# Stick-breaking weights from two sigmoids instead of Abs, Exp, Ln and Exp, one written order over four head pairs, and four gate tiles made as seven-product pairs

## The chip, the cores and the metric

The kernel runs on one core of one Trainium2 chip. The metric is the device time of a run in microseconds; it is given as the median of several runs with the lowest and the highest. A profile is one further execution, recorded by the hardware profiler. The engines are PE (TensorE, with PEld for its weight loads), DVE (VectorE), ACT (ScalarE), POOL (GpSimd) and SP (which issues most of the loads).

## The reference

One layer of a streaming encoder on 1024 prompt rows and 32 sample rows (1056 together), width 1024, all in fp32. One product with `w_in` gives the latents of branch A (latent attention), q, k and v of branch B (stick-breaking attention, 8 heads of 64) and two gates; then come both attentions, the gated merge, and a feed-forward part. The change lies in branch B and in the product with `w_in`:

```python
p = h @ w_in
q_lat, c_kv, k_r, q_b, k_b, v_b, g_a, g_b = jnp.split(p, IN_SPLITS, axis=-1)

def sb_attend(q, qpos, k, v, kpos):
    z = jnp.einsum('bqhd,bshd->bhqs', q, k).astype(jnp.float32) * SB_SCALE
    mask = kpos[None, :] < qpos[:, None]
    sp = jnp.where(mask, jax.nn.softplus(z), 0.0)
    later = lax.cumsum(sp, axis=3, reverse=True) - sp
    a = jnp.where(mask, jnp.exp(jax.nn.log_sigmoid(z) - later), 0.0)
    return jnp.einsum('bhqs,bshd->bqhd', a.astype(v.dtype), v)
```

A weight is thus exp(z - softplus(z) - the sum of softplus over the later keys that are allowed), which is the same number as sigmoid(z) times the product of sigmoid(-z) over those later keys. The prompt's attention takes 1024 queries with 1024 keys; the sample rows take 32 queries with 512 cached keys and their own 32.

## The kernel before

**Products.** Every fp32 operand is held as a high part (rounded to fp32r by ACT, `hi`, L68) and a low part (what is left, by DVE, `lo`, L71), so a product is three matmuls: high by high, low by high, high by low (L75 to L77, or L2207 to L2209 in `prod`). A tile of 128 columns of `w_in` against the 1056 rows is done in one of two ways. Plain: three blocks of 352 rows (`BLK`), 8 x 3 = 24 matmuls each. As a pair: two tiles together as seven products of half-size quarters (`pair`, L595), in the manner of Strassen's scheme; a product is 12 matmuls of 256 and 12 of 272 columns (`HB`), and ACT and DVE make the sums and splits of quarters around it (`half`, `plus`, L538 to L640).

**Stages.** `stage_qkv` makes the first q tile, the first k tile and one latent tile plainly, then the ten others of q, k and v as five pairs. `stage_sb` (L1162) does the prompt's stick-breaking attention for four head pairs, one after the other, and beside it the 16 gate tiles, plainly: 384 steps of three matmuls that fill PE between the pieces of attention. `stage_lat` (L1278) and what stands around it do the other latents, the norms of latents (`lat_norm`, `lat_rstd`, L1236 to L1275) and the sample rows' stick-breaking (`sb_sample`, `sb_weights`, L824 to L842), in two passes of four heads. Then follow the latent attention, merge, and feed-forward.

**Order in SB.** In `stage_sb` PE, ACT and DVE run in a written order (`manual_schedule`), a table of tokens `ORDER` for one head pair, used four times. A token is a letter with a tile: of head `h`, block of 256 queries `u` and half `i`, and behind it `a` or `b` for half a tile. `S` is the scores on PE (L1211, L1212, into PSUM tiles `s`); `a`, `e`, `l`, `E` are the ACT passes Abs, Exp, Ln and Exp (L746, L748, L750, L766); `x`, `c`, `d` are on DVE the maximum with 0 plus the logarithm (L752), the running sum from the last key to the first (L756, L759) and the difference (L764); `k` copies a carry. Then `T` transposes the weights on PE (L807), `h` and `v` split them, `V` multiplies with the values (L821), `o` and `p` gather, and POOL stores the output (L1005). `f` is one step of a gate tile, `W` and `w` split the next weight tile, `G` takes a finished block of a gate tile out of PSUM (L1132) and POOL stores it to the scratch tensor `gd` (L1133). `A`, `D` and `Q` are pieces of a small product for the next norm. Loads of Q, K and V for the next head or pair hang on certain tokens (`then`); they go out on SP.

**Tables of ACT.** The kernel begins with a table of functions that is chosen by name (L130), and ACT changes it only at L1719 and L2352. In `sb_weights` the sample rows go through the same passes (L831 Abs, L832 Exp, L833 Ln, L834 to L841 on DVE, L842 Exp), and each norm of latents takes its inverse root as Identity, Ln, Exp and Square on ACT (L1242 to L1245), then three steps on DVE (L1246 to L1248).

**Buffers.** The weights of the attention lie in tiles with the tag `A` (five buffers); "big" is another tag with three buffers of 1056 numbers, in a pool that lives past SB. `wr`, `wh`, `wl` (the raw weights and their two parts) have two buffers each.

Of the kernel before, what the change touches and what calls it, by code (L numbers as in the profile page):

```python
# [8 lines left out]
F32 = mybir.dt.float32  # L9
# [8 lines left out]
P = 128  # L18
# [26 lines left out]
class K:  # L45
# [82 lines left out]
    def consts(self):  # L128
# [317 lines left out]
    def stage_qkv(self):  # L446
# [3 lines left out]
        nc, a = self.nc, self.a  # L450
        Tp = self.tc.alloc_tile_pool(name="sums", bufs=1, side="right", reuse_waits="tile")
# [58 lines left out]
        def after(kind, p, u):  # L510

            x = u[:, :TP]
            low = x.bitcast(F32R)
            if kind == "q":
                QH = sg() if p == 1 else flat(T4[0])[:, TP * (p - 2) : TP * (p - 1)]
                self.hi(QH, x, 0.125)
                nc.scalar.mul(self.qsb[:, p], u[:, TP:T], 0.125)
                spill("qh", p, QH)
                with self.tc.issue_after(self.plus):
                    stt(low, x, 0.125, fl(QH), ALU.mult, ALU.subtract)  # L520
                spill("ql", p, low)
                return
# [72 lines left out]
        def pair(i, ta, tb, ua, ub):  # L595
# [37 lines left out]
            if i < 4:  # L633
                raws.append((raw(col(*pairs[i + 1][0])), raw(col(*pairs[i + 1][1]))))
# [17 lines left out]
        col = lambda kind, p: 672 + 512 * "qkv".index(kind) + p * P  # L652
        pairs = ((("v", 0), ("v", 1)), (("k", 1), ("q", 1)), (("k", 2), ("k", 3)), (("v", 2), ("v", 3)), (("q", 2), ("q", 3)))
# [34 lines left out]
        self.in_w.append(self.w_in_tile(2208))  # L688
# [27 lines left out]

    def sb_attend(self, score, V, out, fill, then):
        nc = self.nc
        act, vec = nc.scalar.activation, nc.vector
        tiles, banks, seen = {}, {}, {}  # L720
        common = self.sums(V, out, tiles)
        todo = None
        for x in self.ORDER:
            if todo:
                todo()
            todo = then.get(x)
            k, x = x[0], x[1:]
            if k in "fGDQWwA":
                for _ in range(int(x or 1)):
                    fill(k)  # L730
                continue
            h, u = divmod(int(x[0]), 4)
            if k in "SaelxckdE":
                n, i, part = x[0], int(x[2]), x[3:]
                w = (2 * u + i + 1) * P
                m = w // 2 if part else w
                c0 = m if part == "a" else 0
                if k == "S":
                    if part != "b":
                        tiles[x[:3]] = self.tl(self.At, [P, TP], F32, "A")  # L740
                    banks[x] = self.tl(self.ps, [P, 512], F32, "s")
                    score(h, banks[x], 2 * u + i, c0, max(m, 256))
                    continue
                ps, A = banks[x][:, :m], tiles[x[:3]][:, c0 : c0 + m]
                if k == "a":
                    act(A, ps, AF.Abs)  # L746
                elif k == "e":
                    act(A, A, AF.Exp, scale=-1.0)  # L748
                elif k == "l":
                    act(A, A, AF.Ln, bias=1.0)  # L750
                elif k == "x":
                    vec.scalar_tensor_tensor(A, ps, 0.0, A, ALU.max, ALU.add)  # L752
# [14 lines left out]
                continue  # L767
            common(k, x, h, u)
# [264 lines left out]
    def sample_load(self, b):  # L1033

        nc, a = self.nc, self.a
        if b:
# [6 lines left out]
        self.ck, self.cv = self.tl(self.sm2, [P, TP], F32, "A"), self.tl(self.sm2, [P, BIG], F32, "big")  # L1043
        for x, c in ((self.ck, "k"), (self.cv[:, :TP], "v")):
# [54 lines left out]
    def gates(self):  # L1099
# [3 lines left out]
        w, ps, ada = [self.w_in_tile(2208)], [], []  # L1103
# [1650 lines left out]
```

## Time and profile before

| what | us |
|---|---|
| median of 3 runs | 1677.44 |
| lowest, highest | 1676.64, 1681.24 |
| the profiled execution, its span | 1673.5 |
| stage of pairs, 80.6 to 190.5 | 109.9 |
| SB and gates, 190.5 to 500.4 | 309.9 |
| sample rows and latents, 500.4 to 583.0 | 82.6 |

The page and the answers of the trace give no time of the profiled execution other than its span. The boundaries are those that I read from the lines of the first and last instruction of a stage. In a timeline a row is the start in us, the duration in us, the engine, the line, the operation, out<-in, shapes, and in brackets the idle time before with what ended it. In a table of groups, the last columns are busy us, mean ns of one, and idle time before with what ended most of it.

### The profile page before, as it was taken

To read this page: it belongs to the slowest core of one execution; us is meant where nothing else is said; L and a number is where in the kernel's file an instruction comes from. 1 tells how busy PE (TensorE), PEld (TensorE's weight loads), DVE (VectorE), ACT (ScalarE), POOL (GpSimd) and SP (SyncE) were. 2 spreads that over 40 slices of the span, in tenths; PEclk is the share of its full clock that TensorE was granted. 3 is DMA by queue.
4 is the path that set the end of the run, shared out by engine and by line. 5 is a ranking of instruction groups with operands and counts; after the bars stand their busy time and mean duration, and the time that the engine had idled before them with its cause. 6 is when DMAs were issued, how large, how long until landed. Compare 5 with 4: busy or idle time off the path is not lost. (4 is left out here: it accounts for less than half of the span.)

```text
span 1673.5 us, 30264 instructions
## 1 busy us (share of the span) xinstructions
PE 1636.1 (98%) x11592; PEld 1505.2 (90%) x11592; DVE 1268.7 (76%) x2140; ACT 1007.4 (60%) x1945; POOL 297.8 (18%) x581
## 2 busy tenths in 40 slices
PE   5999999999999999999999999999999999999996
PEld 3999999999998889998988799999999999877885
DVE  4865698989873689987765889878778778787455
ACT  4544687978874589887762675544444444454442
POOL 2113312111121221111000212212112111200013
PEclk8999999999999999999999999999999999999998
DMA  9345875576542533222474423432332332796643
GB/s 337 108 131 181 293 232 166 166 198 178 179 126 63 169 105 87 84 87 63 150 256 138 160 89 120 133 133 95 133 133 95 133 133 95 256 331 234 201 141 117
DMA packets 194145, 260.62 MB, mean 156 GB/s; under 512 B 23374, under 2 KB 132304, under 8 KB 193936
## 3 DMA queue, kind: packets, MB, share of 16 engines
q1 hardware_dynamic: 172944, 198.50, 38.2%
q0 software_dynamic: 20688, 59.56, 10.2%
q8 instruction: 91, 1.49, 0.4%
q10 hardware_dynamic: 368, 0.63, 0.1%
q14 instruction: 54, 0.44, 0.1%
HBM read 191.11 MB, written 67.82 MB: 155 GB/s over the span
## 5 line engine op out<-in xcount | busy, mean ns | idle before, releaser
L68 ACT ACTIVATE wh<-wr 128x1024 fp32r<-128x1024 f32 (+2 forms) x151 | 130.1, 864 | 226.6 <-PE s L2208 86.6
L71 DVE TENSOR_TENSOR wl<-wr,wh 128x1024 fp32r<-128x1024 f32 (+2 forms) x151 | 148.5, 986 | 79.3 <-ACT wh L68 79.1
L75 PE MATMUL mm<-hh,wh 128*128 128x352 f32 x456 | 152.6, 335 | 0.0
L76 PE MATMUL mm<-hl,wh 128*128 128x352 f32 x456 | 148.7, 326 | 0.0
L77 PE MATMUL mm<-hh,wl 128*128 128x352 f32 x456 | 148.4, 326 | 0.0
L2207 PE MATMUL mm<-T,wh 128*128 128x256 f32 (+1 forms) x376 | 108.3, 288 | 0.0
L2209 PE MATMUL mm<-T,wl 128*128 128x256 f32 (+1 forms) x376 | 107.3, 286 | 0.4 <-DVE wl L71 0.2
L2208 PE MATMUL mm<-T,wh 128*128 128x256 f32 (+1 forms) x376 | 106.8, 284 | 0.0
L2209 PE MATMUL s<-T,wl 128*128 128x256 f32 (+1 forms) x348 | 99.4, 286 | 0.0
L2207 PE MATMUL s<-T,wh 128*128 128x256 f32 (+1 forms) x348 | 99.4, 286 | 0.0
L2208 PE MATMUL s<-T,wh 128*128 128x256 f32 (+1 forms) x348 | 98.9, 284 | 0.0
L71 DVE TENSOR_TENSOR wl<-S,wh 128x1024 fp32r<-128x1024 f32 (+1 forms) x55 | 59.2, 1078 | 51.8 <-ACT wh L68 51.4
L75 PEld LDWEIGHTS mm<-hh,wh 128*128 128x128 f32 x456 | 86.5, 190 | 3.3 <-issue 2.1
L76 PEld LDWEIGHTS mm<-hl,wh 128*128 128x128 f32 x456 | 86.5, 190 | 2.4 <-issue 0.8
L2348 DVE SCALAR_TENSOR_TENSOR u<-u,c,u 128x1058 f32<-128x1058 f32 x68 | 87.1, 1318 | 2.0 <-ACT u L2345 0.7
L807 PE MATMUL tr<-c,A 128*128 128x128 f32 x576 | 87.2, 272 | 0.0
L77 PEld LDWEIGHTS mm<-hh,wl 128*128 128x128 f32 x456 | 86.4, 189 | 0.2
L68 ACT ACTIVATE wh<-S 128x1024 fp32r<-128x1024 f32 (+1 forms) x55 | 51.8, 943 | 47.6 <-PE s L2208 13.0
L2207 PE MATMUL tr<-T,wh 128*128 128x272 f32 (+1 forms) x272 | 77.9, 286 | 0.0
L2209 PE MATMUL tr<-T,wl 128*128 128x272 f32 (+1 forms) x272 | 77.7, 286 | 0.0
L2208 PE MATMUL tr<-T,wh 128*128 128x272 f32 (+1 forms) x272 | 77.4, 284 | 0.0
L2338 POOL COPY c<-u 128x2 f32<-128x2 f32 x44 | 26.7, 607 | 263.5 <-DVE u L2284 227.6
(770 smaller groups left out, 5832.5 us busy)
## 6 DMA issues: line engine op xcount, KB each, us to landing
wr<-in_w_up_dram SPq DMA_DIRECT2D x44, 512.0 KB, 4.0
dr<-in_w_down_dram SPq DMA_DIRECT2D x43, 512.0 KB, 5.0
wr<-in_w_in_dram SPq DMA_DIRECT2D x33, 512.0 KB, 6.3
A<-in_w_ada_dram SPq DMA_DIRECT2D x32, 512.0 KB, 5.8
wr<-gdn SPq DMA_DIRECT2D x30, 512.0 KB, 4.5
gdn<-u POOLq DMA_DIRECT2D x23, 512.0 KB, 4.9
gd<-nat POOLq DMA_DIRECT2D x48, 176.0 KB, 3.6
t<-gd SPq DMA_DIRECT2D x16, 528.0 KB, 5.1
```

The costliest lines, as they stand in the source:

```text
L68: self.nc.scalar.activation(out, in_, AF.Identity, scale=scale)
L71: return self.nc.vector.tensor_tensor(out, full, hi.bitcast(F32), ALU.subtract)
L75: m(ps, lh, rh, start=start, stop=False)
L76: m(ps, lh, rl, start=False, stop=False)
L77: self.pe = m(ps, ll, rh, start=False, stop=stop).ins
L807: self.nc.tensor.transpose(tr[:, (2 * s + q) * P : (2 * s + q + 1) * P], at[q][:, b * P : b * P + P], self.idt)
L2207: m(ps[:, :n], w[0][:, k], x[0][:, k, c], start=first and k == 0, stop=False, skip_group_check=True)
L2208: m(ps[:, :n], w[0][:, k], x[1][:, k, c], start=False, stop=False, skip_group_check=True)
L2209: i = m(ps[:, :n], w[1][:, k], x[0][:, k, c], start=False, stop=k == 3, skip_group_check=True)
L2338: nc.gpsimd.tensor_copy(self.CV[:, 0:2, cc], u[:, 1024:1026])
L2348: nc.vector.scalar_tensor_tensor(y, u[:, w : w + YW], self.cvT[:, w, cc : cc + 1], y, ALU.mult, ALU.add)
```

## The change

**Sigmoids.** In SB two ACT passes read the scores from PSUM: sigmoid(z) into the tile `A` and sigmoid(-z) into a second tile `rest` with the tag "big". The running sum becomes a running product from the last key to the first (a constant tile `one`, zero with an identity in it, both starts it and keeps it at 1 up to the mask). One multiplication of `A` with the tile `rest`, shifted by one key, gives the weight. For the shift the column behind the last key is set to 0 by a POOL memset, one for each of the 64 tiles. The letters `l`, `x`, `k`, `E` are gone; `a`, `e`, `c`, `d` remain. The sample rows' `sb_weights` and the norms keep their Abs, Exp and Ln.

**One order.** `ORDER` is one table for all four head pairs, so that the pieces of two pairs can mix; a token carries its pair. The loads of Q and K (`L`), and V (`Y`), and of other things (`F`, `Z`) are tokens of their own; `B` replaces a step that hung on the gate blocks. All of these stand at new places.

**Gates.** `GATES = 4`: gate tiles 0 to 3 are made in `stage_qkv` as two more pairs, between the pairs (v2, v3) and (q2, q3), and each is stored whole to `gd` by POOL. The tiles 4 to 15 stay in SB as 288 steps.

```diff
+        self.one = cv.bitcast(BF16)
+        nc.vector.memset(self.one, 0.0)
+        nc.vector.tensor_copy(self.one[:, 384:512], self.idt)
...
+            if kind == "g":
+                self.gsent = nc.gpsimd.dma_start(self.gd[p], u).ins
+                return
...
-        pairs = ((("v", 0), ("v", 1)), (("k", 1), ("q", 1)), (("k", 2), ("k", 3)), (("v", 2), ("v", 3)), (("q", 2), ("q", 3)))
+        pairs = [(("v", 0), ("v", 1)), (("k", 1), ("q", 1)), (("k", 2), ("k", 3)), (("v", 2), ("v", 3))]
+        pairs += [(("g", m), ("g", m + 1)) for m in range(0, self.GATES, 2)]
+        pairs.append((("q", 2), ("q", 3)))
...
+    GATES = 4
...
-        S0.0 a0.0 f1 S0.1 f1 a0.1 e0.0 S1.0 f1 l0.0 f1 e0.1 f1 a1.0 l0.1 e1.0 f1 x0.0 c0.0 f1 d0.0 E0.0 f2 S2.0a
...
-                if k == "a":
-                    act(A, ps, AF.Abs)
-                elif k == "e":
-                    act(A, A, AF.Exp, scale=-1.0)
-                elif k == "l":
-                    act(A, A, AF.Ln, bias=1.0)
-                elif k == "x":
-                    vec.scalar_tensor_tensor(A, ps, 0.0, A, ALU.max, ALU.add)
...
-                elif k == "d":
-                    vec.tensor_tensor(A, ps, A, ALU.subtract)
                 else:
-                    act(A, A, AF.Exp)
...
+            elif k == "a":
+                act(tiles[p][t][:, c], banks[x][:, :m], AF.Sigmoid)
+            elif k == "e":
+                if (p, t) not in rest:
+                    rest[p, t] = self.tl(self.sm2, [P, BIG], F32, "big")
+                    nc.gpsimd.memset(rest[p, t][:, w : w + 1], 0.0)
+                act(rest[p, t][:, c], banks[x][:, :m], AF.Sigmoid, scale=-1.0)
+            elif k == "c":
+                R = rest[p, t]
+                r = R[:, c][:, ::-1]
+                if part == "b":
+                    vec.tensor_tensor_scan(r, r, r, R[:, m : m + 1], ALU.mult, ALU.bypass)
                 else:
+                    vec.tensor_tensor_scan(r, r, self.one[:, 512 - m : 512][:, ::-1], 0.0, ALU.mult, ALU.add)
+            else:
+                A = tiles[p][t][:, c]
+                vec.tensor_tensor(A, A, rest[p, t][:, c0 + 1 : c0 + m + 1], ALU.mult)
...
-            for m in range(16):
+            for m in range(self.GATES, 16):
```

By the order of the instructions the rows of PE go from 10702 to 10750 (288 matmuls of 352 columns fewer, 336 of 256 or 272 more), those of ACT from 1773 to 1601, of DVE from 2104 to 1996, of POOL from 547 to 604 (64 memsets more; 36 stores of blocks and four of whole tiles in place of 48 of blocks), and ACT's loads of a table from 3 to 13. Behind SB the rows of PE and DVE are as before.

The first place is ACT in the first pass of the sample rows, in the stage behind SB. `A` holds the weights of the sample rows, `wr` and `wh` the next weight tile, `lt` and "big" a latent. Before:

```order
L831 ACTIVATE A_6330<-s_6322 128x272
L831 ACTIVATE A_6330<-s_6325 128x272
L832 ACTIVATE A_6330<-A_6330 128x272 x2
L833 ACTIVATE A_6330<-A_6330 128x272 x2
L68 ACTIVATE wh_6376<-wr_6374 128x1024
L68 ACTIVATE wh_6620<-wr_6618 128x1024
L842 ACTIVATE A_6330<-A_6330 128x272
L1304 COPY lt_6245<-s_6347 128x352
L1269 ACTIVATE big_6560<-lt_6245 128x352
L842 ACTIVATE A_6330<-A_6330 128x272
```

Now (the lines count 40 more, those of the latents 53 more):

```order
L871 ACTIVATE A_6175<-s_6167 128x272
L871 ACTIVATE A_6175<-s_6170 128x272
L872 ACT_TABLE_LOAD
L872 ACTIVATE A_6175<-A_6175 128x272 x2
L873 ACT_TABLE_LOAD
L873 ACTIVATE A_6175<-A_6175 128x272 x2
L68 ACTIVATE wh_6221<-wr_6219 128x1024
L1357 COPY lt_6090<-s_6192 128x352
L68 ACTIVATE wh_6465<-wr_6463 128x1024
L1322 ACTIVATE big_6405<-lt_6090 128x352
L882 ACT_TABLE_LOAD
L882 ACTIVATE A_6175<-A_6175 128x272 x2
```

Two loads of a table now stand ahead of the split of the weight tile, and one ahead of the last pass; two of the four other steps changed places.

The second place is ACT in the second pass of the sample rows and the first norm of latents behind it. Before:

```order
L833 ACTIVATE A_6514<-A_6514 128x272 x2
L1269 ACTIVATE nat_6570<-lt_6373 128x352
L842 ACTIVATE A_6514<-A_6514 128x272 x2
L1014 COPY A_6532<-tr_6533 128x512
L1017 COPY A_6532<-tr_6539 32x128
L1242 ACTIVATE A_6581<-mm_6575,c_76 128x264
L1243 ACTIVATE A_6581<-A_6581 128x264
L1244 ACTIVATE A_6581<-A_6581 128x264
```

Now:

```order
L873 ACT_TABLE_LOAD
L873 ACTIVATE A_6359<-A_6359 128x272 x2
L1322 ACTIVATE nat_6415<-lt_6218 128x352
L882 ACT_TABLE_LOAD
L882 ACTIVATE A_6359<-A_6359 128x272 x2
L1054 COPY A_6377<-tr_6378 128x512
L1057 COPY A_6377<-tr_6384 32x128
L1295 ACTIVATE A_6426<-mm_6420,c_76 128x264
L1296 ACT_TABLE_LOAD
L1296 ACTIVATE A_6426<-A_6426 128x264
L1297 ACT_TABLE_LOAD
L1297 ACTIVATE A_6426<-A_6426 128x264
```

The steps stand as before, with a load of a table ahead of every one of these groups of Ln and of Exp.

The third place is POOL at the start of SB, where `ptd` are two constant tiles, `gd` the gates' scratch, `nat` a finished gate block, `ob` the output of a head and "big" the tiles of sigmoid(-z). Before:

```order
L1159 MEMSET ptd_2211 128x128
L1159 MEMSET ptd_2212 128x128
L1133 DMA gd<-nat_2327 128x352
L1133 DMA gd<-nat_2366 128x352
L1005 DMA ob_2181<-o_2436 64x256
L1133 DMA gd<-nat_2475 128x352
```

Now:

```order
L1203 MEMSET ptd_2649 128x128
L1203 MEMSET ptd_2650 128x128
L797 MEMSET big_2740 128x1
L797 MEMSET big_2743 128x1
L797 MEMSET big_2774 128x1
L1175 DMA gd<-nat_2708 128x352
L797 MEMSET big_2780 128x1
L797 MEMSET big_2808 128x1
L1175 DMA gd<-nat_2802 128x352
L797 MEMSET big_2848 128x1
L797 MEMSET big_2855 128x1
L797 MEMSET big_2900 128x1
```

The memsets of new tiles stand in one queue with the stores of gate blocks.

More of the change, by code (lines that the diff above doesn't have):

```diff
@@ L632, in pair @@
             w5 = half(s2b)
-            if i < 4:
+            if i < len(pairs) - 1:
                 raws.append((raw(col(*pairs[i + 1][0])), raw(col(*pairs[i + 1][1]))))
@@ L715, with sb_attend @@
+        3S7.1b 3v7.3 3V6.1 3a7.1b f 3e7.1b Z 3V6.0 f 3c7.1b 3o6 f 3T7.2 3p6 3d7.1b f 3h7.2 3V7.3 3v7.2 3T7.1 3V7.2
+        3h7.1 3T7.0 3v7.1 f 3h7.0 f 3v7.0 3V7.1 B 3V7.0 Q f 3o7 3p7 G
     """.split()
-    def sb_attend(self, score, V, out, fill, then):
+    def sb_attend(self, score, common, fill, load):
         nc = self.nc
         act, vec = nc.scalar.activation, nc.vector
-        tiles, banks, seen = {}, {}, {}
-        common = self.sums(V, out, tiles)
-        todo = None
+        tiles, banks, rest = [{} for _ in range(4)], {}, {}
+        common = [f(tiles[p]) for p, f in enumerate(common)]
@@ L723, in sb_attend @@
         for x in self.ORDER:
[L724 to L730, printed above, removed]
+            if not x[0].isdigit():
+                for _ in range(int(x[1:] or 1)):
+                    fill(x[0])
+                continue
+            p, k, x = int(x[0]), x[1], x[2:]
+            if k in "LY":
+                load(k, p, int(x))
@@ L1031, in pv_sample, with sample_load @@
                                       pv[64 * h : 64 * h + 64, 32 * h : 32 * h + 32])
-    def sample_load(self, b):
+    def sample_load(self, b, part="kv"):
         nc, a = self.nc, self.a
-        if b:
+        if b and part == "k":
             x = self.tl(self.sm2, [P, TP], F32, "A")
@@ L1042, in sample_load @@
         hs = slice(4 * b, 4 * b + 4)
-        self.ck, self.cv = self.tl(self.sm2, [P, TP], F32, "A"), self.tl(self.sm2, [P, BIG], F32, "big")
-        for x, c in ((self.ck, "k"), (self.cv[:, :TP], "v")):
+        for c in part:
+            if c == "k":
+                x = self.ck = self.tl(self.sm2, [P, TP], F32, "A")
+            else:
+                self.cv = self.tl(self.sm2, [P, BIG], F32, "big")
+                x = self.cv[:, :TP]
             self.load(x.rearrange("p (t c) -> p t c", t=4),
@@ L1119, in steps @@
                             yield
-                    if b == 1 and self.ada_sum is not None:
-                        ada.append(self.ada_turn())
                     yield
@@ L1201, in stage_sb @@
                 self.tl(self.sm2, [P, w], F32, g)
-        self.ahead = self.gate_raw(1)
+        self.ahead = self.gate_raw(self.GATES + 1)
         self.sent = self.wlast
@@ L1214, in stage_sb, with fill, load, common @@
         fill = self.gates()
-        E = mybir.EngineType
-        for p in range(4):
-            then = {"S2.0a": lambda: queries(p, 1), "S2.1a": lambda: values(p, 1)}
-            if p == 0:
-                then["S2.1a"] = lambda: (values(p, 1), self.ada_fetch(4, self.sm2))
-            if p < 3:
-                then.update({"S3.1b": lambda: queries(p + 1, 0), "V3.0": lambda: values(p + 1, 0)})
-            with self.tc.manual_schedule(engines={E.PE, E.Activation, E.DVE}):
-                self.sb_attend(score, lambda b, h: V[h][:, b * P : b * P + P], self.store(self.obd[p]), fill, then)
+        gate = fill
+        def fill(k):
+            if k == "F":
+                self.ada_fetch(4, self.sm2)
+            elif k == "Z":
+                self.sample_load(1, "v")
+            else:
+                gate(k)
+        def load(k, p, h):
+            (queries if k == "L" else values)(p, h)
+        def common(p):
+            return lambda tiles: self.sums(lambda b, h: V[h][:, b * P : b * P + P], self.store(self.obd[p]), tiles)
+        E = mybir.EngineType
+        with self.tc.manual_schedule(engines={E.PE, E.Activation, E.DVE}):
+            self.sb_attend(score, [common(p) for p in range(4)], fill, load)
         self.in_w.append(self.next_w.pop(0))
```

131 lines of the change are left out of this document (79 added, 52 removed).

## The prediction

> **What bounds the kernel now.** I read the page first, then the table of stages, then the groups of ScalarE (ACT) and VectorE (DVE), then the timeline at the places that the change touches. The page's own lines on the span and on TensorE (PE):
>
> ```profile
> span 1673.5 us, 30264 instructions
> PE 1636.1 (98%) x11592; PEld 1505.2 (90%) x11592; DVE 1268.7 (76%) x2140; ACT 1007.4 (60%) x1945; POOL 297.8 (18%) x581
> ```
>
> The span is 1673.5 us; the median of the three runs is 1677.44 us (1676.64 to 1681.24), so 3.9 us lie around the span, and I carry them along unchanged. PE is busy 98% of the span, so a change counts here if it takes work off PE or makes PE wait. The stages that the change touches, in the table of stages (length of the stage, then busy time of PE, weight loads, DVE, ACT, POOL, then the granted clock and the DMA share): the products for q, k and v in pairs; stick-breaking (SB); the sample rows and the latents.
>
> ```profile
> 80.60:190.50 109.90, 109.90 (x911) 109.56 (x910) 63.61 (x107) 50.90 (x110) 29.56 (x50) 1.00 0.56 172
> 190.50:500.40 309.90, 309.90 (x2244) 297.31 (x2243) 268.64 (x470) 257.79 (x564) 60.88 (x116) 1.00 0.65 189
> 500.40:583.00 82.60, 81.33 (x622) 73.23 (x620) 40.62 (x85) 41.19 (x86) 16.19 (x32) 1.00 0.40 111
> ```
>
> In the first two PE is busy from end to end at the full clock. DVE is at 87% and ACT at 83% in SB, and yet PE never stands still for them. So what the sigmoids save on ACT and DVE is worth nothing by itself: it only pays if it lets PE do less. The third stage is another matter. ACT is busy there for only half of the time, but it works in chains whose end PE waits for.
>
> **The sigmoids.** Four ACT passes and three DVE passes for a piece of weights become two and two. The groups of before in SB:
>
> ```profile
> L748 ACT ACTIVATE A<-A 128x384 f32<-128x384 f32 (+5 forms) x96 | 50.3, 524 | 1.1
> L746 ACT ACTIVATE A<-s 128x384 f32<-128x384 f32 (+5 forms) x96 | 46.8, 488 | 15.1 <-PE s L1212 14.7
> L752 DVE SCALAR_TENSOR_TENSOR A<-s,A 128x384 f32<-128x384 f32 (+5 forms) x96 | 52.7, 549 | 18.7 <-ACT A L750 18.3
> ```
>
> A sigmoid read from PSUM stands in no row; the nearest are 488 ns (the pass that reads PSUM) and 524 ns (one that doesn't), and I take 488. The other two passes of before (L750, L766) have the same shapes, so ACT loses four passes of some 47 to 50 us and gains two of 47: about 100 us less in SB. DVE loses the 52.7 us of the maximum; the scan and the last step stay, with a product in place of a sum or a difference. Both leave PE's path as they found it, at 0 us. What covers that is PE's own queue; if the cover were gone, the new wait would be a rival (below).
>
> **Four gate tiles in pairs.** Here PE's work changes. A gate tile was three blocks of 24 matmuls of 352 columns. Two of them become seven products of 24 matmuls, 12 of 256 columns and 12 of 272. PE's rows in the timeline, one block of 352 columns behind some transposes, and one product:
>
> ```profile
> 501.18 0.41 PE L75 MATMUL s<-hh,wh 128*128 128x352 f32 x1
> 501.42 0.32 PE L76 MATMUL s<-hl,wh 128*128 128x352 f32 x1
> ...
> 504.97 0.32 PE L77 MATMUL s<-hh,wl 128*128 128x352 f32 x1
> ...
> 101.09 0.28 PE L2207 MATMUL mm<-hh,wh 128*128 128x256 f32 x1
> ...
> 102.53 0.29 PE L2207 MATMUL mm<-hh,wh 128*128 128x272 f32 x1
> ...
> 104.03 0.28 PE L2207 MATMUL s<-hh,wh 128*128 128x256 f32 x1
> ```
>
> The second column must not be used as the price, since neighbours overlap. From start to start, 22 steps of 352 columns take 504.97 - 501.42 = 3.55 us, so 161 ns each; a product takes 104.03 - 101.09 = 2.94 us. Two gate tiles cost 144 x 0.161 = 23.2 us, a pair 7 x 2.94 = 20.6 us. Two pairs save 2 x 2.65 = 5.3 us on PE. The pairs' splits and sums on ACT and DVE lie beside that: in the first stage they are busy 46% and 58%, and the pairs there with more work behind them (v and k go out in natural order) leave PE no gap. The four larger stores of gates sit on POOL's queue, which has the same number of bytes to send as before.
>
> The first matmul behind a transpose takes 0.24 us to the next start (501.18 to 501.42), 0.08 more than the others. By the order of the instructions PE goes from transposes to such a matmul 73 times in SB, 68 times before: +0.4 us.
>
> **What the sigmoids bring along.** In the order of after, ACT loads a table of functions ten more times: once at the first sigmoid, ahead of the first scores and behind eleven steps of gate matmuls, so hidden (1.3 us of ACT if it were not); and nine times where Exp and Ln come back, five in the two sample passes (L832, L833, L842), four in the two norms of latents (L1243, L1244). Before, one table served all of these. The price of a load, from ACT's timeline at another place, where it also stands between two instructions:
>
> ```profile
> 820.56 0.36 ACT L793 COPY o<-pv 64x256 f32<-64x256 f32 x1 [0.16 <-DVE V L71]
> 820.94 1.28 ACT L1719 ACT_TABLE_LOAD   x1
> 822.24 0.20 ACT L1719 ACTIVATE ss<-c 128x1 f32<-128x1 f32 x1
> ```
>
> 820.94 to 822.24 is 1.30 us; the overlap that two ACT instructions otherwise have (about 0.1 us) goes too, so I take 1.4 us a load. The Trainium skill (page "ScalarE: Activation LUTs", section "What ACT_TABLE_LOAD costs") puts a switch at 2.66 us, as 1.28 us of load and 1.38 us of draining; by that the stalls below would double. The 20 ns between the load's end and the next start do not show such a drain.
>
> First sample pass, ACT's rows, DVE's, PE's:
>
> ```profile
> 506.21 0.76 ACT L831 ACTIVATE A<-s 128x272 f32<-128x272 f32 x2
> 506.87 0.74 ACT L832 ACTIVATE A<-A 128x272 f32<-128x272 f32 x2
> 507.51 0.74 ACT L833 ACTIVATE A<-A 128x272 f32<-128x272 f32 x2
> 508.15 1.05 ACT L68 ACTIVATE wh<-wr 128x1024 fp32r<-128x1024 f32 x1
> ...
> 507.96 0.79 DVE L834 SCALAR_TENSOR_TENSOR A<-s,A 128x272 f32<-128x272 f32 x2 [0.63 <-ACT A L833]
> 508.78 0.73 DVE L836 TENSOR_TENSOR_SCAN A<-A 128x272 f32<-128x272 f32 x1
> 509.42 1.20 DVE L71 TENSOR_TENSOR wl<-wr,wh 128x1024 fp32r<-128x1024 f32 x1
> ...
> 510.68 0.43 PE L77 MATMUL mm<-hh,wl 128*128 128x352 f32 x1
> ```
>
> Behind the passes of the sample rows wait, on ACT, the high half of the next weight tile (508.15) and, on DVE, its low half (509.42), which ends at 510.62. PE uses it at 510.68: there is no slack at all. Two loads lie ahead of both halves in the new order, so 2 x 1.4 = 2.8 us: the low half ends at 513.4 and PE stands 2.8 us. The third load falls where ACT has time, ahead of L842.
>
> Second pass, and the norm behind it:
>
> ```profile
> 529.48 0.75 ACT L833 ACTIVATE A<-A 128x272 f32<-128x272 f32 x2
> ...
> 532.71 0.43 ACT L842 ACTIVATE A<-A 128x272 f32<-128x272 f32 x1 [2.10 <-DVE A L841]
> 533.87 0.43 ACT L842 ACTIVATE A<-A 128x272 f32<-128x272 f32 x1 [0.73 <-DVE A L841]
> ...
> 536.64 0.42 ACT L1244 ACTIVATE A<-A 128x264 f32<-128x264 f32 x1
> 537.78 0.58 ACT L1350 COPY lat<-tr 64x512 f32<-64x512 f32 x1 [0.71 <-PE tr L1349]
> 538.38 0.42 ACT L1245 ACTIVATE A<-A 128x264 f32<-128x264 f32 x1
> ...
> 539.62 0.43 DVE L1246 TENSOR_TENSOR A<-A 128x264 f32<-128x264 f32 x1
> ...
> 534.36 0.66 PE L1013 MATMUL tr<-c,A 128*128 128x128 f32 x4
> ...
> 548.11 0.33 PE L75 MATMUL mm<-hh,wh 128*128 128x352 f32 x1
> 548.98 0.44 PE L1320 MATMUL tr<-c,lt 128*128 128x128 f32 x2 [0.55 <-DVE lt L1276]
> ```
>
> One load ahead of L833 delays the whole chain 1.4 us (the one ahead of L842 fits into the 2.10 us in which ACT waits). L842 ended at 534.30 and PE's transposes began at 534.36, so PE stands 1.4 us. In the norm two loads put 2.7 us between L1242 and L1244; ACT had 0.7 us ahead of L1350, and L1246 came 0.8 us behind the end of L1245 (538.80), so about 1.2 us reach the end of the chain, which PE already waits for at 548.98 today. I take 1.0 us of it. Behind the second norm stands nothing that PE needs soon; I take 0. Sum of the stalls: 2.8 + 1.4 + 1.0 = 5.2 us, from 4.2 (without the third) to 6.4 (with 1.2 us more behind the second norm).
>
> **One order, and POOL.** The new order and its buffers can make PE wait in SB. Every sigmoid tile now wants one of three "big" buffers, and a POOL memset in it:
>
> ```profile
> L1133 POOL DMA_DIRECT2D gd<-nat x48 | 26.9, 559 | 126.8 <-ACT nat L1132 116.8 <-ACT A L748 8.3 <-ACT A L746 1.5
> L1159 POOL MEMSET ptd<- 128x128 f32 x2 | 0.4, 225 | 0.0
> ```
>
> The nearest row for the memset is 225 ns. 64 of them stand in POOL's queue between stores that take 559 ns to issue, and each waits for the step that frees its buffer; behind it on POOL wait the next stores, and on ACT the second sigmoid of that tile. The bounds are 0 (PE's own work cannot shrink through it) and, if 40 of the 64 reach PE with their 225 ns, 9 us. I take 0.5, near the lower end, as PE did not wait in SB with ACT and DVE far fuller.
>
> **Sum.** 1673.5 - 5.3 + 0.4 + 5.2 + 0.5 = 1674.3 us of span, and 1678.2 us with the 3.9 around it: the PE time won by the pairs is given back by the table loads.
>
> **Rivals.** *Loads hidden.* If the loads cost PE at most 1 us, the time is 1677.4 - 5.3 + 0.4 + 0.5 to 1.0, 1673 us, and 1672 with no stall at all. For it: ACT is only half busy in that stage. Against it: the three places above have 0.06 us of slack or none. Chance 0.17. The Trainium skill (same page, section "Table sets: the hidden batching unit") says that one set holds both Exp and Ln, so that going from one to the other needs no load; then a single load of 1.4 us would be exposed. The order of after shows loads between them.
>
> *POOL decides (slower).* The memsets stand behind stores that wait for DVE's last sum of a block, so ACT's second sigmoid, the scan and PE's transposes come late, time after time. From about 4 us of such waits on the result is slower; with 5 to 9 us it is 1683 to 1687. For it: the ring has three buffers, and two tiles of a block are in flight at once. Against it: the second sigmoid usually has a first one, or a piece of weights, ahead of it on ACT. Chance 0.17.
>
> *A load costs double.* If each also held ACT for its own length again, the stalls would be about 5.6 + 2.8 + 3 = 11.4 us and the time 1684. The gap of 20 ns speaks against it. Chance 0.05. The 2.66 us of the Trainium skill (the page named above) would lead here.
>
> *The pairs save nothing.* If a matmul of 256 or 272 columns cost its row's 0.28 to 0.29 us, 336 of them would cost 96 us against 288 x 0.32 = 92, and the time would be about 1687. The start-to-start steps speak against it. Chance 0.03.
>
> **Numbers.** The forecast has 0.58: 1676.7 to 1681. A measurement of this kernel can tell about 0.3% (5 us) from no change, so it counts as the same, as does most of the hidden-loads case; only its lower end, and a pair that saves more than I count, is faster: 0.12. Slower: 0.17 + 0.05 + 0.03 = 0.25. Same: 0.63. The range of 1672.3 to 1685 leaves out the far ends of both.
>
> **What would show it.** Stage of pairs 41 us longer, SB about 46 us shorter, PE without a gap in both; ACT in SB near 55%. In the sample stage nine table loads of 1.28 us, and PE gaps of about 2.8 us at L77 behind the first pass, 1.4 at the transposes of the second, 1.7 ahead of L1320. I am wrong if PE has no such gaps, or gaps of its own in SB ended by ACT or POOL, or if a pair takes far from 20.6 us.

## The result, and the profile after

The changed kernel takes 1722.07 us (median of 4 runs, 1718.8 to 1722.56), the kernel before 1678.31 us beside it (4 runs, 1676.64 to 1681.24): 1.0255 times as long, with a 95% interval of 1.0241 to 1.0270. It is slower by 44 us where I forecast no change. The profiled execution took 1718.8 us; its page begins:

```profile
span 1717.0 us, 30312 instructions
PE 1650.8 (96%) x11640; PEld 1508.7 (88%) x11640; DVE 1235.0 (72%) x2042; ACT 937.4 (55%) x1777; POOL 299.1 (17%) x637
```

PE is busy for 15 us more, and the span grew by 43.5 us: most of the loss is PE standing still. The table of stages, with the same columns as before and cuts at three instructions that both kernels have: from the first product of the pairs to the last, from there to the first latent block of the next stage (PE, L75 into `s`, at 501.18 us before), from there to the first scores of latent attention. First after, then before where the cut is new:

```profile
82.67:233.62 150.95, 150.95 (x1248) 150.59 (x1247) 82.97 (x141) 65.25 (x142) 33.25 (x57) 1.00 0.55 165
233.62:535.08 301.46, 278.22 (x1963) 258.45 (x1961) 215.09 (x337) 162.30 (x357) 59.11 (x165) 0.96 0.59 174
535.08:624.53 89.45, 83.23 (x616) 74.10 (x613) 40.39 (x86) 52.46 (x95) 15.90 (x32) 0.98 0.37 102
```

```profile
501.18:583.10 81.92, 80.66 (x617) 72.45 (x615) 40.64 (x86) 40.67 (x86) 15.41 (x31) 1.00 0.40 110
```

| stage | before | after | difference | forecast |
|---|---|---|---|---|
| up to the pairs | 80.6 | 82.7 | +2.0 | 0 |
| pairs | 109.9 | 150.95 | +41.1 | +41.2 |
| SB and gates | 310.7 | 301.5 | -9.2 | -45.5 |
| sample rows, latents | 81.9 | 89.45 | +7.5 | +5.2 |
| the rest | 1090.4 | 1092.5 | +2.1 | 0 |

The first and the last row are work that the change leaves alone. Their instructions are the same. In the first, up to 1.7 of the 2.0 us can be clock: PE was at half of it from 23.3 to 33.6 us before and from 25.8 to 39.5 us after, 3.4 us longer. On the 2 us of the last row I put no cause. The loss is in SB. Without 288 matmuls of 161 ns each (four gate tiles) it would be 310.7 - 46.4 = 264.3 us long; it is 37.2 us longer than that. The granted clock in its row is 0.96, where it was 1.00. The waits of PE in SB (who waits for whom: us in total, how often, the longest):

```profile
PE tr L847 <- DVE ptd L71: 7.2, 1, 7.2
PE s L1254 <- ACT big L798: 6.5, 2, 4.8
PE pv L861 <- DVE ptd L71: 5.6, 2, 4.5
PE pv L861 <- ACT ptd L68: 1.4, 1, 1.4
```

Six waits hold nearly all of it. DVE and ACT are named, but they are 71% and 54% busy there; so the question is what they waited for. The longest, at 333 us, in the timelines of PE, DVE, POOL and SP:

```profile
333.19 0.32 PE L77 MATMUL mm<-hh,wl 128*128 128x352 f32 x1
340.75 1.12 PE L847 MATMUL tr<-c,A 128*128 128x128 f32 x4 [7.24 <-DVE ptd L71]
...
339.20 0.42 DVE L247 TENSOR_TENSOR ada<-ada,mm 128x256 f32<-128x256 f32 x1 [7.11 <-DMA ada<-in_b_ada_dram]
...
340.14 0.55 DVE L71 TENSOR_TENSOR ptd<-tr,ptd 128x384 fp32r<-128x384 f32 x1
...
330.27 1.98 POOL L231 DMA_DIRECT2D ada<-in_b_ada_dram  x4
...
329.53 0.59 SPq L83 DMA_DIRECT2D Q<-ql  x1
330.17 1.24 SPq L83 DMA_DIRECT2D KL<-kl  x2
331.51 0.57 SPq L83 DMA_DIRECT2D wr<-in_w_in_dram  x1
332.13 2.53 SPq L83 DMA_DIRECT2D A<-in_w_ada_dram  x4
```

DVE stands at one addition (L247, the token D) for the load of a bias row, which POOL issued at 330.27 us in the token A; the weights' multiplication and the split that PE needs queue behind it. DVE could start 8.9 us after the first issue; Q, K, a weight tile and four ada tiles (weights of that small product) were on their way at the same time. In the new order A stands a few steps behind the loads of a head, and D a few steps behind A: DVE was at D at 332.09 us (339.20 less 7.11), 1.8 us after the first issue. The wait of 4.5 us at 460 us is the same one for the next rows. The first wait, at 240 us:

```profile
236.91 1.05 POOL L481 DMA_DIRECT2D ql<-fq  x2 [0.73 <-DVE fq L524]
244.81 0.17 POOL L797 MEMSET big<- 128x1 f32 x3 [5.95 <-DMA ql<-fq]
...
244.91 0.55 ACT L798 ACTIVATE big<-s 128x128 f32<-128x128 f32 x2 [4.93 <-DMA ql<-fq]
...
245.25 0.80 PE L1254 MATMUL s<-KH,Q 128*128 128x512 f32 x1 [4.85 <-ACT big L798]
```

The tiles "big" lie in memory that held the last q pair (`fq`), whose low half is still being stored; only when that store has landed may the first sigmoid(-z) be written. The other three (at 392, 417 and 419 us) have one form: ACT's split of a gate tile's weights waits for their load, and the next steps of ACT, on which PE hangs, queue behind it:

```profile
416.57 1.06 ACT L68 ACTIVATE wh<-wr 128x1024 fp32r<-128x1024 f32 x1 [3.06 <-DMA wr<-in_w_in_dram]
...
418.55 0.38 PE L861 MATMUL pv<-ptd,V 128*128 128x256 f32 x1 [1.39 <-ACT ptd L68]
```

Then the clock. Stretches of 2 us around the wait at 333 us, with the granted clock as the third column from the end:

```profile
334.00:336.00 2.00, 0.00 (x0) 0.00 (x0) 0.00 (x0) 0.20 (x1) 0.00 (x0) 1.00 1.01 218
336.00:338.00 2.00, 0.00 (x0) 0.00 (x0) 0.00 (x0) 0.00 (x0) 0.00 (x0) 0.61 1.13 206
...
346.00:348.00 2.00, 2.00 (x12) 2.00 (x12) 1.24 (x3) 0.65 (x2) 0.00 (x0) 0.83 0.00 0
```

Some 3 us after PE fell silent its clock went to half, and it came back at 346.7 us (0.83 in the last row), 5.9 us after work had begun again: 3.0 us more are lost behind the gap. The three long gaps have such a tail each (5.9, 5.9 and 4.7 us at half), which costs 8.3 us in all. The Trainium skill (page "TensorE: Matmul & The Clock Gate", section "Part 1: The HAM clock gate (the "warmup" mystery)") says that the gate knows only half and full rate and decides by a free-running window of 3413 ns. The trace agrees: the clock's loss, summed over each dip in finer stretches, is 3.4, 5.1 and 3.4 us here and 1.7 us in some of the experiments, which is two, three, two and one such windows at half.

So SB's 37.2 us are: six gaps of 21.7 us together (5.2, 7.6, 4.8, 2.0, 1.7 and 1.5 from start to start, less six ordinary steps), 8.3 us of half clock behind three of them, and 7.2 us that no single wait over 0.7 us explains.

In the next stage the nine loads of tables are there as forecast. ACT's rows of the first sample pass, then PE's behind it and at the other two places:

```profile
540.89 1.28 ACT L872 ACT_TABLE_LOAD   x1
542.18 0.75 ACT L872 ACTIVATE A<-A 128x272 f32<-128x272 f32 x2
542.95 1.28 ACT L873 ACT_TABLE_LOAD   x1
...
544.90 1.04 ACT L68 ACTIVATE wh<-wr 128x1024 fp32r<-128x1024 f32 x1
...
545.99 0.43 PE L75 MATMUL mm<-hh,wh 128*128 128x352 f32 x1 [1.59 <-ACT wh L68]
...
547.43 0.43 PE L77 MATMUL mm<-hh,wl 128*128 128x352 f32 x1 [0.85 <-DVE mn L879]
...
571.54 0.65 PE L1286 MATMUL mm<-big,c 128*32 128x264 f32 x8 [1.31 <-DVE mn L879]
...
589.17 0.44 PE L1373 MATMUL tr<-c,lt 128*128 128x128 f32 x2 [0.89 <-DVE lt L1329]
```

### The profile page after: what moved, and what is told of

Same layout as the page of the kernel before. It is cut to its first block, busy times and chain, and to the rows that moved or that the text cites. A ratio compares the mean times of both kernels' runs of the same rounds, so it can differ in the third digit from the quotient of the medians.

```text
span 1717.0 us, 30312 instructions
## 1 busy us (share of the span) xinstructions
PE 1650.8 (96%) x11640; PEld 1508.7 (88%) x11640; DVE 1235.0 (72%) x2042; ACT 937.4 (55%) x1777; POOL 299.1 (17%) x637
## 5 line engine op out<-in xcount | busy, mean ns | idle before, releaser
L68 ACT ACTIVATE wh<-wr 128x512 fp32r<-128x512 f32 (+3 forms) x155 | 130.9, 847 | 232.0 <-PE s L2261 84.2
L71 DVE TENSOR_TENSOR wl<-wr,wh 128x512 fp32r<-128x512 f32 (+3 forms) x155 | 150.3, 973 | 90.1 <-ACT wh L68 89.6
L75 PE MATMUL mm<-hh,wh 128*128 128x352 f32 x360 | 123.9, 344 | 2.2 <-ACT wh L68 1.6
L2262 PE MATMUL mm<-T,wl 128*128 128x272 f32 (+1 forms) x424 | 120.8, 285 | 0.4 <-DVE wl L71 0.2
L77 PE MATMUL mm<-hh,wl 128*128 128x352 f32 x360 | 119.2, 331 | 0.8 <-DVE mn L879 0.8
L847 PEld LDWEIGHTS tr<-c,A 128*128 128x128 f32 x576 | 70.2, 143 | 16.6 <-DVE ptd L71 8.5
L68 ACT ACTIVATE PTh<-tr 128x512 fp32r<-128x512 f32 x96 | 57.6, 601 | 47.8 <-PE tr L847 34.9
L71 DVE TENSOR_TENSOR PTl<-tr,PTh 128x512 fp32r<-128x512 f32 x96 | 65.4, 683 | 22.8 <-ACT PTh L68 21.7
L2260 PEld LDWEIGHTS mm<-T,wh 128*128 128x128 f32 x424 | 79.8, 188 | 1.3 <-ACT wh L68 1.2
L2262 PEld LDWEIGHTS mm<-T,wl 128*128 128x128 f32 x424 | 79.9, 189 | 1.1 <-DVE wl L71 1.1
L2261 PEld LDWEIGHTS mm<-T,wh 128*128 128x128 f32 x424 | 79.8, 188 | 0.0
```

The lines of the kernel that those rows point to most:

```text
L68: self.nc.scalar.activation(out, in_, AF.Identity, scale=scale)
L71: return self.nc.vector.tensor_tensor(out, full, hi.bitcast(F32), ALU.subtract)
L75: m(ps, lh, rh, start=start, stop=False)
L77: self.pe = m(ps, ll, rh, start=False, stop=stop).ins
L847: self.nc.tensor.transpose(tr[:, (2 * s + q) * P : (2 * s + q + 1) * P], at[q][:, b * P : b * P + P], self.idt)
L2260: m(ps[:, :n], w[0][:, k], x[0][:, k, c], start=first and k == 0, stop=False, skip_group_check=True)
```

## The experiments

My theory after the traces (theory 1): the sigmoids and the pairs do what they should, and the loss is the named waits, each paid again in half clock. Its rivals: the new order is too tight everywhere, so that another wait takes each place; or the clock falls by itself. All ratios are to the kernel before, run beside.

**e1, the bias row one step earlier.**

```diff
-            self.acc = self.tl(tp, [P, 256], F32, "ada")
-            self.ada_bias(v)
+            self.acc = self.acc_next
+        if v < 5 and self.ada_todo[0][1] == 4:
+            self.acc_next = self.tl(tp, [P, 256], F32, "ada")
+            self.ada_bias(v + 1, self.acc_next)
```

> Edit: in the changed kernel, the four small loads of a bias row set (b_ada, issued by POOL) go out one ada step (A) earlier, into a buffer of their own; nothing else. Theory 1 (single waits, each paid twice): PE's gaps of 7.4 us at 333 us and 4.6 us at 460 us exist because DVE stands at L247 for this load, which lands 5 to 8 us behind its issue while Q, K and weight loads fill the DMA engines, and PE's granted clock is 0.5 for 6.0 and 4.7 us of work behind them (3.0 and 2.3 us more). Then both gaps and both dips go: 1722 - 17 = about 1705 us. Rival 2 (the new order is too tight everywhere): another wait takes each place, the time stays above 1717 us. Rival 3 (the low clock comes from the work, not from the gap): only the 12.0 us go, 1710 us, and the clock still shows dips near 340 and 465 us.

1710.25 us, ratio 1.0204 (1.0185 to 1.0223), where theory 1 had 1705. SB is 294.3 us: 7 us shorter than in the changed kernel, not 17. DVE's waits at L247 for the load are gone, and so is the gap at 460 us. But at 337 us PE stands for 3.1 us, and ACT says why:

```profile
340.61 0.74 PE L864 MATMUL pv<-ptd,V 128*128 128x256 f32 x4 [3.08 <-DVE o L838]
...
337.91 1.06 ACT L68 ACTIVATE wh<-wr 128x1024 fp32r<-128x1024 f32 x1 [3.19 <-DMA wr<-in_w_in_dram]
```

Behind the wait for the bias stood the wait for a weight tile, which the first had hidden. The rival is half right.

**e2, the low half of the last q pair in a buffer of its own.**

```diff
+                if p > 1:
+                    low = sg()
                 with self.tc.issue_after(self.plus):
                     stt(low, x, 0.125, fl(QH), ALU.mult, ALU.subtract)
```

> Edit: in the changed kernel, the low half of the last q pair is written into a buffer of its own (sg) instead of over its source in fq, so that the tiles of sigmoid(-z), which lie in the same memory as fq, don't wait for its store to DRAM. Theory 1: PE's gap of 5.0 us at 240 us and the 5.9 us of half clock behind it (3.0 us) go: 1722 - 8 = about 1714 us. Rival: the first sigmoids are late in any case (the table load, and the loads of K behind the store of q's high half), and the gap shrinks by less than 2 us: 1719 us or more.

1716.65 us, ratio 1.0244 (1.0221 to 1.0267), not told apart from the changed kernel's 1.0255, and less than the 8 us that theory 1 gave it. The gap at 240 us is gone without a trace, but 2.4 us appear at 261 us, again behind a weight tile that came late, with one window of half clock. SB is 297.9 us, 3.5 us shorter.

**e3, one load of the table that has both Exp and Ln, behind SB.**

```diff
             self.sb_attend(score, [common(p) for p in range(4)], fill, load)
+            nc.scalar.preload_act_table_set("natural_log_exp_and_others")
```

> Edit: in the changed kernel, one load of the table that serves both Exp and Ln, chosen by name, stands behind the last step of SB on ACT; the nine loads in the sample passes and norms are gone. Theory 1: the stage of the sample rows gets back what it lost, 41.4 - 33.9 = 7.5 us, nearly all: 1722 - 7 = about 1715 us. Rival (the loads were hidden, and the stage is longer for another reason): 1719 us or more.

1710.9 us, ratio 1.0200 (1.0175 to 1.0225). The stage of the sample rows takes 82.0 us up to 617.00, and its first instruction of latent attention starts at 616.72:

```profile
534.98:617.00 82.02, 81.12 (x618) 72.80 (x616) 40.87 (x86) 40.72 (x86) 15.96 (x32) 1.00 0.42 113
```

That is 81.7 us to the same cut, as before (81.9); SB is unchanged. So the nine loads cost 7.5 us, all of it in that stage. (The ratio fell by 0.0055, some 9 us, but that difference is known only to about 5 us.) The Trainium skill (page "ScalarE: Activation LUTs", section "Table sets: the hidden batching unit") says that one set holds both functions; the run agrees once that set is loaded by name, and the loads between Exp and Ln in the changed kernel show that it was not the set taken there.

**e4, the three together.**

> Edit: the edits of e1, e2 and e3 together. Theory 1 (the waits are independent of each other): the three gains add up, 17 + 8 + 7 = 32 us, 1690 us; what is then left against the kernel before (1678) is the waits for gate weights at 392 and 417 us and small ones, less the gain of the pairs. Rival 2 (order too tight): less than half of the sum comes, above 1706 us.

1698.77 us, ratio 1.0126 (1.0103 to 1.0150): 22 us came, not 32. The gains do add up: singly the ratio fell by 0.0051, 0.0011 and 0.0055, together by 0.0129, and SB is 10.1 us shorter where it was 7.1 and 3.6 us shorter singly. What falls short of theory 1 are e1 and e2 themselves, since each uncovers late weights. What was left, at its worst place (SP, ACT, PE):

```profile
400.54 1.23 SPq L83 DMA_DIRECT2D KL<-kl  x2
401.97 0.43 SPq L83 DMA_DIRECT2D wr<-in_w_in_dram  x1
...
406.57 1.06 ACT L68 ACTIVATE wh<-wr 128x1024 fp32r<-128x1024 f32 x1 [5.60 <-DMA wr<-in_w_in_dram]
...
408.55 0.39 PE L866 MATMUL pv<-ptd,V 128*128 128x256 f32 x1 [3.93 <-ACT ptd L68]
```

The gate tile's weights are asked for behind six loads of Q and K. ACT was at the split at 400.97 us (406.57 less 5.60), 1.0 us before SP issued the load.

**e7, and the gate weights asked for a tile earlier.** On top of e4:

```diff
-                        if m > self.GATES:
-                            raw.append(self.gate_raw(m + 1))
...
                 w[0] = tuple(v(x) for x in w[0])
+                if more:
+                    raw.append(self.gate_raw(more.pop(0)))
```

> Edit: e4 (bias early, q's low half apart, one table) and the load of a gate tile's raw weights issued one tile earlier, as soon as the buffer of its predecessor has been split. Theory 1: the gaps that are left in e4 (4.3, 3.5, 2.4, 2.3 and 1.5 us at 404, 332, 259, 380 and 409 us) all stand behind ACT's split of weights that waits for its load behind Q and K loads on SP's queue; they go with some 5 us of half clock: 1699 - 19 = about 1680 us. Rival 2 (order too tight): other waits take their place, above 1690 us.

1681.6 us, ratio 1.0016 (1.0004 to 1.0028). No wait of PE in SB is over 0.4 us by the list of waits, and the clock is full:

```profile
233.01:505.51 272.50, 269.73 (x1962) 250.95 (x1961) 214.31 (x337) 163.13 (x358) 58.84 (x165) 1.00 0.66 193
```

Four edits of loads, stores and tables, none of arithmetic, take back 40 of the 44 us. SB is 8.2 us longer than 264.3. PE stands idle for 2.8 us of that by the row; that the rest are shorter waits still is not shown here.

**e5, the sigmoids alone, in the order of before with all 16 gate tiles.**

```diff
-                    act(A, ps, AF.Abs)
+                    act(A, ps, AF.Sigmoid)
...
-                    act(A, A, AF.Exp, scale=-1.0)
+                    if t not in rest:
+                        rest[t] = self.tl(self.sm2, [P, BIG], F32, "big")
+                        nc.gpsimd.memset(rest[t][:, w : w + 1], 0.0)
+                    act(rest[t][:, c], ps, AF.Sigmoid, scale=-1.0)
```

> Edit: the kernel before, with the sigmoids alone: its own order of one head pair (the letters l, x, k and E do nothing), 16 gate tiles in SB, no gate pairs. Theory 1 (the new order is what costs SB, not the sigmoids): PE has no waits of over 1 us in SB behind its first 10 us; the nine table loads cost 7 us in the sample stage and the first sigmoid(-z) waits for the store out of fq (up to 5 us and 3 of half clock): 1683 to 1692 us. Rival B (the sigmoids, their memsets on POOL or the scores held longer in PSUM stop PE all through SB): above 1700 us.

1701.06 us, ratio 1.0135 (1.0118 to 1.0152). That is above my range and just above the rival's bound, but the mechanism is not the rival's: PE has one wait in SB,

```profile
PE s L1206 <- ACT big L752: 8.7, 1, 8.7
```

the one at the start for the store out of `fq`, longer here because the old order has fewer fill steps ahead of it. Its step of 9.0 us and the half clock behind it make SB 10.5 us longer than before; all the rest of it, with 64 memsets and 192 sigmoids, runs as before. The sample stage is 9.5 us longer, 2.0 us more than in the changed kernel, for which I have no cause.

**e6, the pairs alone.** Abs, Exp, Ln and Exp as before, four gate tiles in pairs, and the old order with every fourth fill step left out:

```diff
-        S0.0 a0.0 f1 S0.1 f1 a0.1 e0.0 S1.0 f1 l0.0 f1 e0.1 f1 a1.0 l0.1 e1.0 f1 x0.0 c0.0 f1 d0.0 E0.0 f2 S2.0a
+        S0.0 a0.0 S0.1 f a0.1 e0.0 S1.0 f l0.0 f e0.1 a1.0 l0.1 e1.0 f x0.0 c0.0 f d0.0 E0.0 f S2.0a
```

> Edit: the kernel before, with the gate pairs alone: four gate tiles as two pairs in the q/k/v stage, Abs, Exp, Ln, Exp as before, and its order of one head pair with every fourth fill step (and the matching G, W, w) left out. Theory 1: the pairs save 5 us of PE, but PE in SB falls to 264 us while DVE needs 269 and ACT 258 us there, so DVE bounds the stage, with waits and half clocks: 1680 to 1700 us. Rival (PE still bounds it): 1671 us.

1702.65 us, ratio 1.0146 (1.0130 to 1.0161), above the range of theory 1. SB takes 291.9 us with DVE busy for 259 of them and PE waiting for it again and again:

```profile
231.60:523.51 291.91, 275.35 (x1962) 251.23 (x1961) 259.16 (x465) 247.05 (x547) 51.53 (x98) 1.00 0.61 179
```

```profile
PE s L1216 <- DVE A L770: 11.5, 16, 0.9
```

The pairs need the sigmoids: without them DVE sets the pace. The half clocks that theory 1 expected did not come: PE has the full clock all through SB.

**e8 and e9, both ideas in the old order.** e6 with the sigmoids, one table, the q half apart and the weights early (e8), then with the first ada step of a head pair later and one fill step moved (e9):

```diff
-        T2.2 k3.0a d3.0a A h2.2
+        T2.2 k3.0a d3.0a h2.2
...
-        p2 V3.3
+        p2 A V3.3
```

> Edit: the kernel before with both ideas of the change and without its new order: sigmoids and four gate tiles in pairs, the order of one head pair with every fourth fill step left out, one table load behind SB, q's low half apart, weights early. Theory 1: the ideas are sound and the placing of loads was not; 1676 - 5.3 for the pairs + 1.5 for the table at the start: about 1672 us. Rival (the sigmoids or the pairs have a cost of their own): above 1680 us.

1682.5 us, ratio 1.0025 (1.0015 to 1.0036): on the rival's side, not theory 1's 1672. PE stands three times between 252 and 257 us, 2.2 us together, for ada weights that have not landed, and once at 513 us.

> Edit: e8 with two steps of its written order moved: the first ada step of a head pair (A, D) ten fill steps later, so that its weights have landed, and one fill step behind the last values (V7.0), by which DVE's split of the weight tile comes ahead of the sample rows' second scan again. Theory 1: the PE gaps of e8 at 252 to 257 us (1.5, 0.9, 1.0 and 0.4 us against 0.3 in an undisturbed step), the one of 1.6 us at 513 us and two windows of half clock (1.7 us each) go: 1682.5 - 6.5 = about 1676 us, 0.1 to 0.4% faster than before. Rival (the order is too tight once PE has less to do): other waits take their place, 1680 us or more.

1680.25 us, ratio 1.0011 (1.0002 to 1.0020), the rival's side again. The waits that e9 was to remove went, the clock is full all through SB, and still it is no faster than before. SB takes 271.7 us, 7.4 us more than 264.3, and the waits of PE in it that have most are for DVE, first:

```profile
234.40:506.06 271.66, 268.27 (x1961) 252.38 (x1961) 215.48 (x337) 164.50 (x358) 58.24 (x163) 1.00 0.66 192
```

```profile
PE tr L810 <- DVE A L769: 1.8, 2, 0.9
```

**e10, eight tiles in pairs.** As e9, with `GATES = 8` and half of the fill steps:

> Edit: as e9 (without its step behind V7.0), with eight gate tiles in pairs instead of four, and half of the fill steps of before in SB. Theory 1: each pair saves PE 2.65 us, but PE in SB falls to 214 us, and DVE, which was busy for 214 us of the changed kernel's SB, becomes its bound: the gain of 5.3 us is eaten by short waits, 1672 to 1682 us, with no window of half clock as long as the waits stay under 2 us. Rival (PE still bounds SB): 1671 us or less.

1693.51 us, ratio 1.0096 (1.0078 to 1.0113), worse than either theory. SB takes 246.65 us where 310.7 - 576 x 0.161 = 217.9 would be left: 28.7 us lost, some 5 of them by three windows of half clock.

```profile
275.49:522.14 246.65, 228.95 (x1674) 210.31 (x1673) 210.00 (x333) 153.44 (x341) 50.49 (x149) 0.98 0.67 193
```

```profile
PE pv L823 <- DVE ptd L71: 9.1, 5, 2.1
```

With the old order and 16, 12 and 8 gate tiles in SB the loss against PE's own work is 0 (e5, behind its start), 7.4 (e9) and 28.7 us (e10), while a pair wins 2.65 us each time. The fill steps were not idle weight: with fewer of them PE stands for DVE's chain from scores to weights. None of the versions is faster than the kernel before.

## Why the prediction was wrong, point by point

- **The pairs** were right: 41.06 us for two where I said 41.2, and PE without a gap in that stage at 1.00.
- **The sigmoids** were right in what they free: ACT is at 54% of SB (I said near 55), and a sigmoid took 494 ns from PSUM into `A` and 504 ns into "big" by the groups, where I took 488. e5 shows that behind its start they cost PE nothing in the old order. What I left out is the memory of their second tiles: the wait for the store out of `fq` comes with the sigmoids and not with the new order, since e5 has it too, with a step of 9.0 us.
- **The table loads** were right in mechanism and near in size: 5.2 us forecast, 7.5 measured. From start to start the first pass cost PE 2.8 us, as I had it (idle times of 1.59 and 0.85 us in the rows), the second 1.4 as I had it, the norm some 0.3 where I had 1.0. The place of the second was wrong: PE stood at L1286 (571.54 us), whose input DVE makes behind the step that waits for L873, 2.5 us ahead of the transposes that I named. What I left out was the clock, one window of half rate behind the first wait, 1.7 us, and the second norm, which I put at 0: PE is 40.2 us later than before at 589.78 us and 41.4 us later at 624.53 us, so 1.2 us more. That is 7.4 us together. A load took 1.28 us and the next pass began 10 to 20 ns later, as the row at L1719 had said; the 2.66 us of the Trainium skill (page "ScalarE: Activation LUTs", section "What ACT_TABLE_LOAD costs") did not show here either.
- **"One order, and POOL"** is the step that failed: "I take 0.5, near the lower end, as PE did not wait in SB with ACT and DVE far fuller." It measured 37.2 less the 0.4 that I counted for transposes. I bounded the memsets' price and took it for the price of the whole rewrite. The order also moved every load, and I looked at each engine's share of busy time and not at what each load had ahead of it and how soon its user came. In the table of tokens I should have set A against L, and W against its load. Why PE did not wait before shows in the rows of the bias loads in SB, before and after (the last number is the median time from issue to landing, in us):

```profile
ada<-in_b_ada_dram POOLq DMA_DIRECT2D x12, 32.0 KB, 2.1
```

```profile
ada<-in_b_ada_dram POOLq DMA_DIRECT2D x12, 32.0 KB, 6.3
```

Two things changed: the loads land later, and their user comes sooner. Before, DVE came to the addition at 294.73 us, 5.3 us after the first issue (289.40) and without a wait for the load; now it is there after 1.8 us.

- **The memsets** cost 0.10 us each, not 0.225, and only the first one held PE, through its memory and not through POOL's queue. So the rival "POOL decides" had the right sign and place of stop (ACT's second sigmoid), and a wrong mechanism; it also gave 1687 at most.
- **The missing price** was that of a gap: 2.3 to 3.0 us lost to half clock behind each of three gaps. PE had no gap in these stages before, but the start of that same trace shows the price: behind waits of 0.5 to 0.8 us from 19 us on, and in one of 1.9 us, PE went to half clock at 23.3 us for 10.2 us.

```profile
23.00:34.00 11.00, 8.38 (x34) 6.33 (x36) 8.79 (x14) 9.20 (x17) 4.23 (x8) 0.53 1.05 378
```

- What stays open: the last 7.2 us of SB are many waits of under 0.7 us, most of them without a name in the list of waits. e9 and e10 point to the number of fill steps; I did not try a shorter DVE chain, which would be the proof.

## What to carry to other kernels

When an order is rewritten, list for each load what is issued ahead of it and how many microseconds later its user stands in line, and do so for loads of a few kilobytes too: the user blocks all that is queued behind it on its engine. A saving on PE counts only as far as the other engines' chains stay covered by what PE still does. A version of a change that fails as a whole can still be sound in its parts, and taking out one wait brings less than its length where another stands behind it (7 us of 17 in e1).

## What the runs showed of the hardware

The clock of PE fell to half behind gaps shorter than I would have thought, and not always. In e10 four equal steps of 2.35 to 2.37 us occur, one in each head pair; behind three of them one window of half clock follows, behind the one at 412.6 us none (stretches around two of them, the clock third from the end):

```profile
292.00:294.00 2.00, 0.35 (x3) 0.11 (x1) 2.00 (x4) 1.13 (x3) 0.57 (x1) 1.00 1.03 412
294.00:296.00 2.00, 1.56 (x6) 1.56 (x7) 1.90 (x4) 0.00 (x0) 0.09 (x1) 0.58 1.02 387
...
412.00:414.00 2.00, 0.91 (x6) 0.65 (x4) 2.00 (x3) 1.35 (x4) 0.47 (x1) 1.00 0.00 0
414.00:416.00 2.00, 1.02 (x7) 1.02 (x8) 2.00 (x4) 0.00 (x0) 0.72 (x4) 1.00 0.32 107
```

Nor does the longer gap always lose more: in e4 a step of 3.5 us (332.42 to 335.93) has no half clock behind it, as the rows show, one of 2.4 us (259.07 to 261.44) has a window.

```profile
334.00:336.00 2.00, 0.07 (x1) 0.07 (x1) 1.67 (x3) 1.60 (x4) 0.05 (x1) 1.00 1.04 408
336.00:338.00 2.00, 2.00 (x15) 1.98 (x16) 0.47 (x1) 0.00 (x0) 1.02 (x2) 1.00 0.99 394
```

Steps of up to 1.25 us, many times in SB of e6, had none. Yet in e7 one window at half clock, from 527.0 to 530.4 us, follows the small products of the sample rows (L1072, 64 columns), where PE's longest wait was 0.6 us. So the length of a gap alone does not decide; what else does is not shown here. The Trainium skill (page "TensorE: Matmul & The Clock Gate", section "Part 1: The HAM clock gate (the "warmup" mystery)") puts the fall behind at least one idle window of about 3.4 us; here 2.4 us were enough three times in four, and the measurement decides.

A load that POOL issues is no way around loads that SP has issued: the bias rows, 32 KB each, took up to 7.7 us to land in the changed kernel. The Trainium skill (page "DMA: Bandwidth & Descriptors", section "Issuing engines are not separate DMA queues") says that all issuers share the same engines and interleave there; the rows of landing times above, 2.1 and 6.3 us, agree.
